# A second norm whose sample columns go through VectorE, a layer set-up that comes earlier, and scalings tied to set steps

## The chip, the cores and the metric

The kernel runs on one core of one Trainium2 chip. The time is that of the device for one execution, in microseconds (us). A core has five engines with instruction streams of their own: TensorE (PE in the profile, with its weight loads shown apart as PEld), VectorE (DVE), ScalarE (ACT), GpSimd (POOL) and SyncE (SP, which here only issues DMAs). Each works through its own stream strictly in order. An instruction that waits for another engine or for a DMA holds up all that stands behind it on its engine.

## The reference

Two layers over 512 prompt tokens and 8 samples of 8 tokens each (64 sample columns), width 1024. Layer 1 is a gated delta rule, layer 2 a differential attention in which keys and values are shared and the samples also read pages of a cache. Around the change this is computed:

```python
def modulate(x, gain, shift, scale):
    return rms_norm(x, gain) * (1 + scale[:, None, :]) + shift[:, None, :]

x = x + gate[:, None, :] * y                     # end of layer 1 (output projection, residual)
h = modulate(x, norm_kv, shift, scale)           # input of k and v
k, v = split(h @ w_kv)
h = modulate(x, norm_b, shift, scale)            # input of q and z
q, z = split(h @ w_in_b)
q = partial_rotary(rms_norm(q), cos, sin)        # the same for k
```

Shift, scale and gate are vectors over the width. The prompt has one set of them, each of the eight samples has its own: so the 512 prompt columns need one scalar per channel, the 64 sample columns a small table of eight per channel.

## The kernel before, in words

Activations lie with channels on the 128 partitions: a tensor such as `x1` is 128 x 8 channel tiles x 576 columns (512 prompt, 64 sample). Every projection is done in two halves of 288 columns; the sample columns are the last 64 of the second half. An operand is split into a high and a low part (`hhi`, `hlo` for activations, `whi`, `wlo` for weights), and three products of the parts are summed (`part`, L238), so one output tile of 128 channels and one half takes 8 x 3 = 24 matmuls. Weights come by SP into `wraw` (L214), ACT rounds them to `whi` (L217), POOL takes the difference `wlo` (L218), about one tile ahead.

The work around the change runs in this order of the program:

1. `out_a` (L1722) finishes the output projection of layer 1, half 0 and then half 1, adds the residual into `x1`, squares it on ACT (L1747), sums the squares on DVE into `rstd` (L1749). `rstd` sits in one of four buffers (`pg`) that later take cache pages.
2. `norm(half)`, inside `out_a`: the sum over partitions on PE (L1731), the reciprocal root by twelve DVE operations (`rsqrt_to`, L181 to L188), and `modulate` (L350), which writes `hhi` and `hlo` for one half. Per channel tile DVE scales (L360), ACT adds the shift and rounds (L362), DVE takes the low part (L363). In the second half each channel tile's 64 sample columns go through three POOL operations (L368 to L370), an ACT copy (L371) and a POOL difference (L372). `norm(0)` runs inside the projection; `norm(1)` is called by `phase_b`.
3. `phase_b` (L2089) starts with the layer's set-up: constants, identity and causal mask in bf16, the lambda of the attention, gains, page table. It has six DMAs on SP and some short DVE, POOL and ACT operations. Then come the cosine and sine tables times the gains (L2156).
4. q projection. Four q tiles (`QH`) get their half 0, with `norm(1)` behind the first; then one block does half 1 of all four, channel tile by channel tile, so 8 x 4 x 3 = 96 matmuls. Four more q tiles follow whole. Every tile is finished by `QKTile.finish`: transposes on PE (L1805, L1807), a copy, squares on ACT (L1810), a sum and a reciprocal root on DVE (L1811 to L172), the rotary part on POOL (L1819 to L1822), transposes back (L1826, L1828), and a last copy to `qT` on ACT and DVE (L1830). Buffers let two finishes run at a time and four tiles wait for theirs.
5. Between the finishes stand three scalings, at places given by `PRE`: `x1` times `rstd` (L2180), the kv input `kT` from it (`scale_shift`, L375, lines L380, L383, L384), and the second use of the q input for z, in place in `x1` (the same lines).
6. `split` (L387) turns `kT` into `hhi` and `hlo` (L393 on ACT, L394 on DVE); then the k tiles, the v tiles and, among them, the samples' pages (`load_page`, L1862, which a POOL copy L1867 and an SP read of its value lead), and the attention.

What sets the order: the first phase's streams are pinned by hand. From `out_a` on a scheduler at compile time orders each engine's stream. It works on simulated time, takes what is ready, and prefers what comes earlier in the program. So a later instruction that is ready stands ahead of an earlier one that isn't, and on the chip that order is fixed. `PRE` therefore gives a place in the program, not a time.

Scratch tiles of 128 x 640 (`scr`) have three buffers in this part.

## Time and profile before

| | |
|---|---|
| time, median of three runs | 1313.99 us (1311.61 to 1315.3) |
| span of the profiled execution | 1313.1 us; it has no other time of its own shown beside the span |
| instructions | 34330 |
| DMA | 240.61 MB, mean 183 GB/s |
| 740 to 760 us (output projection, half 0 and 1) | PE busy 19.11 of 20.00 |
| 800 to 810 us (second norm, second half) | PE busy 6.19 of 10.00, clock 0.56 |
| 840 to 850 us (q tiles) | PE busy 10.00 of 10.00, clock 1.00 |

A row of the timeline gives start and length in us, engine, line, operation, what is written and read with its size, and in brackets how long the engine stood idle before it and who ended that. A matmul's length is that of a pipelined instruction: its successor starts before it ends, so the pace is read from counts over a stretch. In a table of stretches, the columns are the length, then busy time and instruction count of PE, PEld, DVE, ACT and POOL, then the clock granted to PE as a share, the DMA share and GB/s. A row of waits gives the total, the number of times and the longest.

### The profile page before, as it was taken

The numbers are of one execution on the slowest core, as the hardware profiler recorded it, in microseconds if no ns is written. First come the engines' busy times: TensorE is split into PE (matmuls) and PEld (weight loads), VectorE is DVE, ScalarE is ACT, GpSimd is POOL, SyncE is SP. The second block draws the span as 40 slices with busy tenths as digits, with TensorE's granted clock in tenths as the row PEclk, the third lists the DMA queues.
The fourth block names the chain that finished last, engine by engine and source line by source line (L and its number), as shares of the span: only waits on it lengthen the run. The fifth ranks groups of instructions, "written<-read, shape, count | busy, mean of one in ns | idle before, by whom it ended". The sixth has DMA issues, their size and how long they took to land.

```text
span 1313.1 us, 34330 instructions
## 1 busy us (share of the span) xinstructions
PE 1245.7 (95%) x13227; PEld 1083.6 (83%) x13227; DVE 807.7 (62%) x2263; ACT 715.5 (54%) x1981; POOL 444.0 (34%) x811
## 2 busy tenths in 40 slices
...
GB/s 360 133 197 174 157 204 158 195 156 166 200 156 180 153 212 153 189 205 191 226 189 133 163 172 56 81 65 163 297 212 276 213 257 258 284 218 192 93 130 112
DMA packets 86646, 240.61 MB, mean 183 GB/s; under 512 B 14339, under 2 KB 26499, under 8 KB 86483
## 3 DMA queue, kind: packets, MB, share of 16 engines
...
HBM read 212.55 MB, written 25.84 MB: 182 GB/s over the span
## 4 chain that ended last, share of the span: by engine, by line
PE 79%; DVE 6%; DMA 6%; POOL 3%; issue 3%; ACT 2%; SPq 1%; POOLq 0%; DVEq 0%; ACTq 0%
PE pp L437 27%; PE pp L241 14%; PE pa L437 6%; PE pc L437 6%; PE ps L437 2%; PE po L1940 2%; PE pt L437 2%; PE pS L1897 2%; DMA pg<-cv 2%; PE pt L443 2%; PE sc L241 2%; PE pv L2060 1%; DMA pg<-ck 1%; PE sc L2020 1%; DMA araw<-ada 1%
## 5 line engine op out<-in xcount | busy, mean ns | idle before, releaser
L241 PE MATMUL pp<-hhi,whi 128*128 128x288 f32 x640 | 195.0, 308 | 18.8 <-ACT hhi L371 11.9
L241 PE MATMUL pp<-hlo,whi 128*128 128x288 f32 x640 | 193.5, 303 | 2.7 <-DVE hlo L1681 1.9
L241 PE MATMUL pp<-hhi,wlo 128*128 128x288 f32 x640 | 191.7, 301 | 0.2 <-POOL wlo L218 0.2
L437 PE MATMUL pp<-hlo,whi 128*128 128x288 f32 x576 | 166.2, 310 | 0.1
L218 POOL TENSOR_TENSOR wlo<-wraw,whi 128x1024 fp32r<-128x1024 f32 x50 | 120.8, 2419 | 133.3 <-ACT whi L217 115.9
L437 PE MATMUL pp<-hhi,whi 128*128 128x288 f32 x576 | 156.9, 294 | 0.0
L241 PEld LDWEIGHTS pp<-hhi,whi 128*128 128x128 f32 x640 | 121.0, 190 | 27.1 <-ACT hhi L371 12.6
L241 PEld LDWEIGHTS pp<-hlo,whi 128*128 128x128 f32 x640 | 121.7, 190 | 8.1 <-DVE hlo L1681 2.4
L437 PE MATMUL pp<-hhi,wraw 128*128 128x288 f32 x576 | 124.2, 300 | 0.0
L241 PEld LDWEIGHTS pp<-hhi,wlo 128*128 128x128 f32 x640 | 121.7, 190 | 2.3 <-issue 1.7
L437 PEld LDWEIGHTS pp<-hlo,whi 128*128 128x128 f32 x576 | 108.6, 189 | 6.2 <-issue 3.4
L437 PEld LDWEIGHTS pp<-hhi,whi 128*128 128x128 f32 x576 | 108.4, 188 | 0.4
L437 PEld LDWEIGHTS pp<-hhi,wraw 128*128 128x128 f32 x576 | 93.3, 188 | 5.3 <-issue 4.9
L437 PE MATMUL pp<-hhi,wlo 128*128 128x288 f32 x576 | 96.8, 302 | 0.0
L217 ACT CAST whi<-wraw 128x1024 fp32r<-128x1024 f32 x50 | 52.4, 1048 | 77.6 <-PE pp L241 54.4
L970 DVE SCALAR_TENSOR_TENSOR y<-u,vec,y 128x600 f32<-128x600 f32 x96 | 84.9, 884 | 11.4 <-ACT y L967 9.9
L437 PE MATMUL pp<-hlo,wraw 128*128 128x288 f32 x288 | 83.1, 312 | 0.1
L437 PEld LDWEIGHTS pp<-hhi,wlo 128*128 128x128 f32 x576 | 81.2, 188 | 2.1 <-issue 1.2
L790 POOL DMA_DIRECT2D wlo<-wall x37 | 32.9, 889 | 124.2 <-ACT wlo L785 94.3
L2040 DVE TENSOR_REDUCE mx<-sc 128x1 f32<-128x128 f32 (+3 forms) x64 | 31.4, 491 | 60.2 <-PE sc L2022 60.1
L1867 POOL COPY pg<-ptt 1x1 int32<-1x1 int32 x128 | 29.2, 236 | 107.8 <-PE po L1940 46.1
L437 PEld LDWEIGHTS pp<-hlo,wraw 128*128 128x128 f32 x288 | 54.1, 188 | 2.4 <-issue 0.7
...
## 6 DMA issues: line engine op xcount, KB each, us to landing
...
```

The source lines that it names most:

```text
L217: nc.scalar.copy(out=hi[:], in_=raw[:])
L218: nc.gpsimd.tensor_sub(out=lo[:], in0=raw[:], in1=hi[:].bitcast(F32))
L241: K.mm(out=ps[:, :HT], lhsT=w[a][:, k, :], rhs=h[b][:, k, half * HT:half * HT + HT], start=(k == 0 and a + b == 0), stop=(k == 7 and a == 1))
L437: return self.K.nc.tensor.matmul(**kw)
L443: return self.K.nc.tensor.transpose(**kw)
L790: K.nc.gpsimd.dma_start(out=lo[:], in_=src, accum_op=ALU.add)
L970: nc.vector.scalar_tensor_tensor(out=y[:, :YW], in0=u[:, j:j + YW], scalar=cw[j], in1=y[:, :YW], op0=ALU.mult, op1=ALU.add)
L1867: nc.gpsimd.tensor_copy(out=e, in_=P.ptt[0:1, i:i + 1])
L1897: nc.tensor.matmul(out=S[32 * j:32 * j + 32, 128 * pg:128 * pg + 128], lhsT=qs[:, h, :], rhs=kp[:, h, :], start=(hh == 0), stop=(hh == 1), ...
L1940: nc.tensor.matmul(out=po[32 * j:32 * j + 8, hf, :], lhsT=pTs[:, pg, 8 * h:8 * h + 8], rhs=vp[:, h, :], start=False, stop=(pg == NPG - 1 a ...
L2020: nc.tensor.matmul(out=ps[:, :w], lhsT=q[r, m, :], rhs=self.kl[r, 0:w], start=False, stop=False, tile_position=(64 * m, 0))
L2040: nc.vector.tensor_reduce(out=mx[:, m:m + 1], in_=pss[m][:, :w], axis=AX.X, op=ALU.max, negate=True)
```

## The change

Four things are edited.

The second half of the second norm is written by `modulate_rows`. All 8 channel tiles' sample columns together (128 x 512) go through three DVE operations and one ACT copy ahead of the prompt columns, and through a fourth DVE operation behind the first prompt tile. `norm(0)` uses the same function without the sample part. `norm` now returns its last DVE instruction.

The set-up of layer 2 is a function of its own, `setup_b`, called before `out_a`. Two bf16 copies and the memset of `zb` in it are on POOL now, the copies having been on DVE. The cosine and sine tables stay, but are made after `norm(1)`.

Two blocks stand in `tc.issue_after(instruction)`: every instruction traced in the block on that instruction's engine is placed behind it in the stream; no wait is added, and other engines aren't held. The tables go behind the last DVE instruction of `norm(1)`. The three scalings go behind the last DVE instruction (L1830) of the finish of q tile 1, 3 and 6; `PRE` was (1, 5, 6).

`scale_shift` does the sample columns of all channel tiles in two POOL operations in place of sixteen.

```diff
--- before.py
+++ after.py
@@ -372,6 +372,36 @@
                 nc.gpsimd.tensor_sub(out=lo[:, k, SEQ:], in0=tn, in1=hi[:, k, SEQ:].bitcast(F32))
 
 
+def per_sample(t, s):
+
+    return t[:, s, 1:9].unsqueeze(3).to_broadcast([128, 8, NB, DS])
+
+
+def modulate_rows(K, x, rstd, g1, shift_kt, hi, lo, half):
+
+    nc = K.nc
+    n = SEQ - HT if half else HT
+    sl = slice(half * HT, half * HT + n)
+    if half:
+        t = scr(K, 8 * NS).rearrange("p (k n) -> p k n", n=NS)
+        t4 = t.rearrange("p k (b e) -> p k b e", e=DS)
+        nc.vector.tensor_mul(out=t, in0=x[:, :, SEQ:], in1=rstd[:, SEQ:].unsqueeze(1).to_broadcast([128, 8, NS]))
+        nc.vector.tensor_mul(out=t4, in0=t4, in1=per_sample(g1, slice(0, 8)))
+        nc.vector.tensor_add(out=t4, in0=t4, in1=per_sample(K.mod, slice(shift_kt, shift_kt + 8)))
+        nc.scalar.copy(out=hi[:, :, SEQ:], in_=t)
+    for k in range(8):
+        t1 = scr(K, HT)
+        sh = K.mod[:, shift_kt + k, :]
+        nc.vector.scalar_tensor_tensor(out=t1[:, :n], in0=x[:, k, sl], scalar=g1[:, k, 0:1], in1=rstd[:, sl],
+                                       op0=ALU.mult, op1=ALU.mult)
+        nc.scalar.activation(out=hi[:, k, sl], in_=t1[:, :n], func=AF.Identity, bias=sh[:, 0:1])
+        if half and k == 0:
+            nc.vector.tensor_sub(out=lo[:, :, SEQ:], in0=t, in1=hi[:, :, SEQ:].bitcast(F32))
+        last = nc.vector.scalar_tensor_tensor(out=lo[:, k, sl], in0=t1[:, :n], scalar=sh[:, 0:1],
+                                              in1=hi[:, k, sl].bitcast(F32), op0=ALU.add, op1=ALU.subtract)
+    return last
+
+
 def scale_shift(K, xr, g1, shift_kt, out):
 
     nc = K.nc
@@ -379,9 +409,9 @@
         sh = K.mod[:, shift_kt + k, :]
         nc.vector.tensor_scalar(out=out[:, k, 0:SEQ], in0=xr[:, k, 0:SEQ], scalar1=g1[:, k, 0:1], scalar2=sh[:, 0:1],
                                 op0=ALU.mult, op1=ALU.add)
-        xs, os = (a[:, k, SEQ:].rearrange("p (b e) -> p b e", e=DS) for a in (xr, out))
-        nc.gpsimd.tensor_mul(out=os, in0=xs, in1=g1[:, k, 1:9].unsqueeze(2).to_broadcast([128, NB, DS]))
-        nc.gpsimd.tensor_add(out=os, in0=os, in1=sh[:, 1:9].unsqueeze(2).to_broadcast([128, NB, DS]))
+    xs, os = (a[:, :, SEQ:].rearrange("p k (b e) -> p k b e", e=DS) for a in (xr, out))
+    nc.gpsimd.tensor_mul(out=os, in0=xs, in1=per_sample(g1, slice(0, 8)))
+    nc.gpsimd.tensor_add(out=os, in0=os, in1=per_sample(K.mod, slice(shift_kt, shift_kt + 8)))
 
 
 def split(K, t, hi, lo):
@@ -755,7 +785,7 @@
 NV = 0
 WARM = 6
 XW = 2
-PRE = (1, 5, 6)
+PRE = (1, 3, 6)
 SAT = (1, 3, 6)
 FILL = ('vvuv|', 'vvuuu|', 'vuuv|uuuuv', 'huu|', 'zz|u', 'uu|uuzuuu', '|uuuu', 'Zuuuu|zuu', '|uuzZzffff')
 LAST = 'ffffs'
@@ -1730,7 +1760,7 @@
         r = rstd[:, half * HT:half * HT + HT]
         nc.tensor.matmul(out=ps[:, :HT], lhsT=K.ones, rhs=r, start=True, stop=True)
         rsqrt_to(K, r, ps[:, :HT], 1.0 / D, EPS)
-        modulate(K, x1, rstd, K.g1["g1b"], 40, K.hhi, K.hlo, halves=(half,))
+        return modulate_rows(K, x1, rstd, K.g1["g1b"], 40, K.hhi, K.hlo, half)
 
     gain1(K, "norm_b", 48, "g1b")
     with ExitStack() as octx:
@@ -1813,7 +1843,7 @@
         r = rsqrt(K, P.tk, ss[:], 10, tag="rq")
         nc.vector.tensor_mul(out=t[:], in0=t[:], in1=r[:].unsqueeze(2).to_broadcast([128, 10, 64]))
 
-        cos, sin = self.tabs
+        cos, sin = self.tabs[self.out is P.kT]
         rc = P.tk.tile([128, 10, 16], F32, name="rc")
         rsn = P.tk.tile([128, 10, 16], F32, name="rsn")
         nc.gpsimd.tensor_mul(out=rc[:], in0=t[:, :, 0:16], in1=cos)
@@ -1827,15 +1857,15 @@
         pb2 = K.pb.tile([128, 512], F32, name="pb")
         nc.tensor.transpose(out=pb2[:, 0:64], in_=tv[0:64, 4, :], identity=K.ident[0:64, 0:64])
         nc.scalar.activation(out=self.out[:, self.h, :SEQ], in_=pb[:], func=AF.Copy, scale=self.gain)
-        nc.vector.tensor_scalar(out=self.out[:, self.h, SEQ:], in0=pb2[:, 0:64], scalar1=self.gain, scalar2=None,
-                                op0=ALU.mult)
+        return nc.vector.tensor_scalar(out=self.out[:, self.h, SEQ:], in0=pb2[:, 0:64], scalar1=self.gain, scalar2=None,
+                                       op0=ALU.mult).ins
 
 
 def qk_tile(*a):
     t = QKTile(*a)
     t.half(0)
     t.half(1)
-    t.finish()
+    return t.finish()
 
 
 def v_tile(K, P, h):
@@ -2086,43 +2116,34 @@
 LAM_INIT = 0.8 - 0.6 * math.exp(-0.3)
 
 
-def phase_b(K, ctx, x1, rstd, norm_rest):
-    nc = K.nc
-    tc = K.tc
+def setup_b(K, ctx):
+
+    nc = K.nc
     P = Ctx()
-
-    def pool(name, bufs):
-        return ctx.enter_context(tc.tile_pool(name=name, bufs=bufs))
-
-    one = pool("b1", 1)
-    P.pg = K.pg
-    P.ss = pool("bss", 2)
+    one = ctx.enter_context(K.tc.tile_pool(name="b0", bufs=1))
     c = load_con(K, one, K.con_in, "amask", "plain")
     K.comb = c("comb")
     K.m01 = c("m01")
     K.amask = c("amask")
-    K.identb = one.tile([128, 128], BF16, name="identb")[:]
-    nc.vector.tensor_copy(out=K.identb, in_=K.ident)
-    K.cmaskb = one.tile([128, 128], BF16, name="cmaskb")[:]
     cm = scr(K, 128)
     nc.sync.dma_start(out=cm, in_=K.con_in[:, CON["cmask"][0]:CON["cmask"][1]])
-    nc.vector.tensor_copy(out=K.cmaskb, in_=cm)
+    lp = scr(K, 256).rearrange("p (a d) -> p a d", d=64)
+    nc.sync.dma_start(out=lp, in_=K.lp_in.to_broadcast([128, 4, 64]))
+    gc = P.gc = one.tile([128, 2], F32, name="gc")
+    nc.sync.dma_start(out=gc[:], in_=K.gc_in)
+    gr = P.gr = one.tile([128, 2, 16], F32, name="gr")
+    nc.sync.dma_start(out=gr[:], in_=K.gr_in.to_broadcast([128, 2, 16]))
+    P.ptt = one.tile([1, 64], I32, name="ptt")
+    nc.sync.dma_start(out=P.ptt[:], in_=K.pt_in)
+    K.identb = one.tile([128, 128], BF16, name="identb")[:]
+    nc.gpsimd.tensor_copy(out=K.identb, in_=K.ident)
+    K.cmaskb = one.tile([128, 128], BF16, name="cmaskb")[:]
+    nc.gpsimd.tensor_copy(out=K.cmaskb, in_=cm)
+    P.zb = one.tile([128, 128], BF16, name="zb")
+    nc.gpsimd.memset(P.zb[:], 0.0)
     K.sg2 = one.tile([128, 1], F32, name="sg2")
     nc.vector.tensor_scalar(out=K.sg2[:], in0=K.vec[:, VEC["sg"][0]:VEC["sg"][1]], scalar1=0.5 * (1.0 - LAM_INIT),
                             scalar2=None, op0=ALU.mult)
-    P.kT = one.tile([128, 8, NT], F32, name="kT")
-    P.qT = one.tile([128, 8, NT], F32, name="qT")
-    P.qs = [one.tile([128, 8, 32], F32, name=f"qs{i}") for i in range(AHEAD + 1)]
-    P.zb = one.tile([128, 128], BF16, name="zb")
-    for t in P.qs + [P.zb]:
-        nc.gpsimd.memset(t[:], 0.0)
-    P.vn = [one.tile([128, 4, 128], F32, name=f"vn{h}") for h in range(NV)]
-    P.oT = P.qT[:, :, SEQ:].rearrange("p h (b t) -> p h b t", t=8)
-    P.ptt = one.tile([1, 64], I32, name="ptt")
-    nc.sync.dma_start(out=P.ptt[:], in_=K.pt_in)
-
-    lp = scr(K, 256).rearrange("p (a d) -> p a d", d=64)
-    nc.sync.dma_start(out=lp, in_=K.lp_in.to_broadcast([128, 4, 64]))
     l2 = one.tile([128, 4], F32, name="l2")
     nc.vector.tensor_mul(out=lp[:, 0:4:2, :], in0=lp[:, 0:4:2, :], in1=lp[:, 1:4:2, :])
     nc.vector.tensor_reduce(out=l2[:, 0:2], in_=lp[:, 0:4:2, :], axis=AX.X, op=ALU.add)
@@ -2133,37 +2154,53 @@
     P.sgn = one.tile([128, 1], F32, name="sgn")
     nc.vector.scalar_tensor_tensor(out=P.sgn[:], in0=K.m01[:, 1:2], scalar=P.nlam[:, 0:1], in1=K.m01[:, 0:1],
                                    op0=ALU.mult, op1=ALU.add)
-
-    gc = one.tile([128, 2], F32, name="gc")
-    nc.sync.dma_start(out=gc[:], in_=K.gc_in)
-    gr = one.tile([128, 2, 16], F32, name="gr")
-    nc.sync.dma_start(out=gr[:], in_=K.gr_in.to_broadcast([128, 2, 16]))
     for g in (gc[:, 1:2], gr[:, 1, :]):
         nc.vector.tensor_scalar(out=g, in0=g, scalar1=0.125, scalar2=None, op0=ALU.mult)
     nc.vector.scalar_tensor_tensor(out=gc[:], in0=gc[:], scalar=c("plain")[:, 0:1],
                                    in1=c("plain")[:, 1:2].to_broadcast([128, 2]), op0=ALU.mult, op1=ALU.add)
+    return P
+
+
+def phase_b(K, P, ctx, x1, rstd, norm_rest):
+    nc = K.nc
+    tc = K.tc
+
+    def pool(name, bufs):
+        return ctx.enter_context(tc.tile_pool(name=name, bufs=bufs))
+
+    one = pool("b1", 1)
+    P.pg = K.pg
+    P.ss = pool("bss", 2)
+    gc, gr = P.gc, P.gr
+    P.kT = one.tile([128, 8, NT], F32, name="kT")
+    P.qT = one.tile([128, 8, NT], F32, name="qT")
+    P.qs = [one.tile([128, 8, 32], F32, name=f"qs{i}") for i in range(AHEAD + 1)]
+    for t in P.qs:
+        nc.gpsimd.memset(t[:], 0.0)
+    P.vn = [one.tile([128, 4, 128], F32, name=f"vn{h}") for h in range(NV)]
+    P.oT = P.qT[:, :, SEQ:].rearrange("p h (b t) -> p h b t", t=8)
     P.sp = pool("bsp", 1)
     tctx = ExitStack()
     P.tk = tctx.enter_context(tc.tile_pool(name="btk", bufs=2))
     P.ch = tctx.enter_context(tc.tile_pool(name="bch", bufs=QH))
     rot = load_con(K, P.tk, K.con_in, "cos", "sin", 1)
-    tabs = []
-    for i in (1, 0):
-        tab = []
-        for n in ("cos", "sin"):
-            src = rot(n).rearrange("p (c d) -> p c d", d=16)
-            dst = P.tk.tile([128, 10, 16], F32, name=n + "q", bufs=1)[:] if i else src
-            nc.vector.tensor_mul(out=dst, in0=src, in1=gr[:, i, :].unsqueeze(1).to_broadcast([128, 10, 16]))
-            tab.append(dst)
-        tabs.append(tab)
     qctx = ExitStack()
     extra_w(K, qctx, "qx", [("b", h * 128) for h in range(2, QH)])
-    tiles = []
+    tiles, tabs = [], []
     for h in range(QH):
-        tiles.append(QKTile(K, P, ("b", h * 128), h, gc[:, 1:2], tabs[0], P.qT))
+        tiles.append(QKTile(K, P, ("b", h * 128), h, gc[:, 1:2], tabs, P.qT))
         tiles[h].half(0)
         if h == 0:
-            norm_rest()
+            normed = norm_rest().ins
+    with tc.issue_after(normed):
+        for i in (1, 0):
+            tab = []
+            for n in ("cos", "sin"):
+                src = rot(n).rearrange("p (c d) -> p c d", d=16)
+                dst = P.tk.tile([128, 10, 16], F32, name=n + "q", bufs=1)[:] if i else src
+                nc.vector.tensor_mul(out=dst, in0=src, in1=gr[:, i, :].unsqueeze(1).to_broadcast([128, 10, 16]))
+                tab.append(dst)
+            tabs.append(tab)
     pss = [p.tile([128, 512], F32, name=n) for p, n in ((K.pp, "pp"), (K.pp, "pp"), (K.pt, "pt"), (K.pt, "pt"))]
     for k in range(8):
         for t, ps in zip(tiles, pss):
@@ -2172,22 +2209,23 @@
         t.evac(1, ps)
     for h in range(8):
         if h < QH:
-            tiles[h].finish()
+            done = tiles[h].finish()
         else:
-            qk_tile(K, P, ("b", h * 128), h, gc[:, 1:2], tabs[0], P.qT)
-        if h == PRE[0]:
-            for k in range(8):
-                nc.vector.tensor_mul(out=x1[:, k, :], in0=x1[:, k, :], in1=rstd[:])
-        if h == PRE[1]:
-            scale_shift(K, x1, gain1(K, "norm_kv", 32, "g1kv"), 24, P.kT)
-        if h == PRE[2]:
-            scale_shift(K, x1, K.g1["g1b"], 40, x1)
+            done = qk_tile(K, P, ("b", h * 128), h, gc[:, 1:2], tabs, P.qT)
+        with tc.issue_after(done):
+            if h == PRE[0]:
+                for k in range(8):
+                    nc.vector.tensor_mul(out=x1[:, k, :], in0=x1[:, k, :], in1=rstd[:])
+            if h == PRE[1]:
+                scale_shift(K, x1, gain1(K, "norm_kv", 32, "g1kv"), 24, P.kT)
+            if h == PRE[2]:
+                scale_shift(K, x1, K.g1["g1b"], 40, x1)
     samples = [Sample(K, P, b) for b in range(NB)]
     ahead = iter(samples)
     qctx.close()
     split(K, P.kT, K.hhi, K.hlo)
     for h in range(8):
-        qk_tile(K, P, ("kv", h * 128), h, gc[:, 0:1], tabs[1], P.kT)
+        qk_tile(K, P, ("kv", h * 128), h, gc[:, 0:1], tabs, P.kT)
         nc.sync.dma_start(out=K.k_out[h], in_=P.kT[:, h, :])
         if h in SAT:
             next(ahead).pages()
@@ -2396,7 +2434,8 @@
             K.x1p = bctx.enter_context(tc.tile_pool(name="x1p", bufs=1))
             x1 = K.x1p.tile([128, 8, NT], F32, name="x1")
             rstd = K.pg.tile([128, 8, 128], F32, name="pg")[:].rearrange("p a b -> p (a b)")[:, 0:NT]
-            phase_b(K, bctx, x1, rstd, out_a(K, x1, rstd))
+            P = setup_b(K, bctx)
+            phase_b(K, P, bctx, x1, rstd, out_a(K, x1, rstd))
 
 
 def arrays_of(i):
```

## The prediction

> **What bounds the kernel now.** I read the page first: busy time, then the chain that ended last. They say that TensorE (PE) sets the end, so what the change can win is time in which PE stands still or runs at a lowered clock.
>
> ```profile
> PE 1245.7 (95%) x13227; PEld 1083.6 (83%) x13227; DVE 807.7 (62%) x2263; ACT 715.5 (54%) x1981; POOL 444.0 (34%) x811
> PE 79%; DVE 6%; DMA 6%; POOL 3%; issue 3%; ACT 2%; SPq 1%; POOLq 0%; DVEq 0%; ACTq 0%
> ```
>
> So I followed that chain in order of time to where it leaves PE. Between 796 and 826 us it runs through VectorE (DVE) and GpSimd (POOL). The busy time by stage shows the hole and what follows it (columns: length, then busy time of PE, of its weight loads, DVE, ACT and POOL with instruction counts, then clock, DMA share, GB/s):
>
> ```profile
> 796.00:804.00 8.00, 0.47 (x3) 0.33 (x2) 7.79 (x18) 2.20 (x6) 4.75 (x9) 0.67 0.08 33
> 800.00:810.00 10.00, 6.19 (x28) 5.84 (x29) 9.57 (x20) 3.15 (x9) 10.00 (x22) 0.56 0.00 0
> 804.00:827.00 23.00, 17.84 (x97) 16.35 (x97) 15.75 (x31) 5.46 (x16) 22.36 (x58) 0.82 0.00 1
> 827.00:859.00 32.00, 31.17 (x235) 30.35 (x236) 23.27 (x66) 19.10 (x46) 17.23 (x17) 1.00 0.32 99
> ```
>
> The fourth row gives PE's undisturbed pace: 31.17/235 = 0.133 us a matmul. From 796 to 827 PE does 100 matmuls, 13.3 us of work, in 31 us: some 18 us are lost there and only 0.8 in the next 32. Who it waits for, between 788 and 827 and then up to 880 (columns: total, times, longest):
>
> ```profile
> PE pp L241 <- ACT hhi L371: 11.9, 3, 7.5
> PE pt L1807 <- DVE qkt L1808: 1.9, 2, 1.6
> ```
>
> L371 is the copy of the sample columns in the second norm, one per channel tile, behind three POOL operations each. The timelines of the three engines show why it is late:
>
> ```profile
> 789.96 0.45 DVE L181 TENSOR_SCALAR pg<-px 128x288 f32<-128x288 f32 x1
> 791.90 0.29 DVE L2127 TENSOR_TENSOR scr<-scr 128x128 f32<-128x128 f32 x1 [1.50 <-DMA scr<-lp]
> 793.33 0.17 DVE L2142 TENSOR_SCALAR gr<-gr 128x16 f32<-128x16 f32 x1 [0.92 <-DMA gr<-gr]
> 798.16 0.46 DVE L187 TENSOR_TENSOR scr<-scr 128x288 f32<-128x288 f32 x1
> 798.65 0.46 DVE L188 SCALAR_TENSOR_TENSOR pg<-scr,pg 128x288 f32<-128x288 f32 x1
> 804.11 0.50 POOL L383 TENSOR_TENSOR kT<-x,g1kv 128x64 f32<-128x64 f32 x1
> 825.78 0.29 POOL L384 TENSOR_TENSOR x<-x,mod 128x64 f32<-128x64 f32 x1
> 803.67 0.85 PE L241 MATMUL pp<-hhi,whi 128*128 128x288 f32 x2 [7.53 <-ACT hhi L371]
> 826.30 0.29 PE L241 MATMUL pt<-hhi,wlo 128*128 128x288 f32 x1
> ```
>
> Two faults stand in them. The layer's set-up waits for its DMAs in the middle of the reciprocal root (L181 to L188). And from 804 the later scalings (L383, L384 and on DVE L2180, L380) stand between the norm's own steps, since nothing holds them back. After the 7.53 us pause the granted clock is down as well (0.56 in the second row of stages).
>
> **The change part by part.** *Set-up out of the root.* L181 starts at 789.96 and takes a step of 0.37 to its successor; L182 and L183 take 0.3 each, the nine dependent steps 0.49 each (798.16 to 798.65): 5.4 us, so the root is ready at 795.4 and not at 799.1. Gain 3.7 us. If another instruction still slips in, this is 2 us; it can't be below nothing, since the same instructions remain.
>
> *Sample columns in four DVE operations.* Three of 128x512 before the first tile, one after it. The nearest row is 128x640 in 0.82 us (below), so 0.75 each: 2.25 us, then a first scaling, ACT's copy and bias, 0.8 us: PE starts at 798.4. Then DVE needs 2 x 0.43 us a channel tile (the pitch of L360 and L363 there), PE four output tiles x 3 x 0.133 = 1.6 us, so PE sets the pace: 96 x 0.133 = 12.8 us, with 0.8 us for the first low part (among it the fourth operation) ends at 812.0 in place of 826.4. **-14.4 us** for both parts; bounds -16.5 (low parts never late) and -12 (the three operations at a lowered PE clock, 2.4 us).
>
> ```profile
> 805.12 0.49 DVE L360 SCALAR_TENSOR_TENSOR scr<-x,g1b,pg 128x224 f32<-128x224 f32 x1 [0.21 <-POOL hlo L372]
> 851.76 0.82 DVE L1814 TENSOR_TENSOR qkt<-qkt,rqy 128x640 f32<-128x640 f32 x1
> 844.57 0.28 DVE L1830 TENSOR_SCALAR qT<-pb,gc 128x64 f32<-128x64 f32 x1 [1.13 <-PE pb L1828]
> 848.34 0.28 DVE L1830 TENSOR_SCALAR qT<-pb,gc 128x64 f32<-128x64 f32 x1 [0.25 <-PE pb L1828]
> 872.73 0.28 DVE L1830 TENSOR_SCALAR qT<-pb,gc 128x64 f32<-128x64 f32 x1
> 834.65 0.17 DVE L170 TENSOR_TENSOR rqt<-rqy 128x10 f32<-128x10 f32 x1
> 852.50 2.37 DVE L170 TENSOR_TENSOR rqt<-rqy 128x10 f32<-128x10 f32 x1
> 852.26 2.58 POOL L218 TENSOR_TENSOR wlo<-wraw,whi 128x1024 fp32r<-128x1024 f32 x1 [4.61 <-ACT whi L217]
> L2180 DVE TENSOR_TENSOR x<-x,pg 128x576 f32<-128x576 f32 x8 | 6.7, 853 | 0.5 <-POOL scr L368 0.5
> L380 DVE TENSOR_SCALAR kT<-x,g1kv,mod 128x512 f32<-128x512 f32 x8 | 4.1, 537 | 0.0
> 809.66 1.65 DVE L2180 TENSOR_TENSOR x<-x,pg 128x576 f32<-128x576 f32 x2
> 822.75 0.99 DVE L380 TENSOR_SCALAR x<-x,g1b,mod 128x512 f32<-128x512 f32 x2
> DVE qss L1811 <- ACT scr L1810: 5.5, 6, 2.9
> L394 DVE TENSOR_TENSOR hlo<-kT,hhi x16: 445/446/675, 855.3 to 865.8; 128x288 fp32r<-128x288 f32 x16
> 859.08 0.39 ACT L1793 COPY ch<-pp 128x288 f32<-128x288 f32 x1
> ```
>
> *The scalings behind set steps: the cover that goes.* In the hole the scalings (6.7 + 4.1 us on DVE here, 4.1 more for x) cost PE nothing beyond the hole. They now start behind the last DVE instruction of a finish (L1830): x1 times the root behind q tile 1, kT behind tile 3. The kv projection needs kT, and nothing else is left for PE once the eight q tiles are multiplied. That happens at the block's end + 31.5 us (826.4 to 858, when the last q tile's copy at 859.08 is less than a us away and eight kv matmuls are already in): 843.5. When is kT there?
> - Finish of tiles 0 and 1: last L1830 at 848.34, 21.9 after the block; the same chain after the new block: 834.
> - x1 times the root, behind it: 8 steps, 6.4 us at their pitch of 0.80 (two in 1.65), plus one weight split on POOL (L218) beside it. L170 shows what that does: 2.37 us for an operation that takes 0.17 otherwise, as POOL's split runs. 834 + 6.4 + 2.2 = 842.6.
> - Finishes of tiles 2 and 3: in the trace from 848.34 to 872.73, but with 16 splits of kT (L394) and three POOL splits in between. Counting only their own dependent steps (a copy, a square, a reduction, nine root steps of 0.2, a product, 1.9 on POOL, a transpose) it is 9.7 us: 852.3. One more weight split and POOL's merged scalings beside it: 2 to 5 us. I take 855; bounds 845 (finishes at DVE's pace, no collision) and 861 (every collision in full).
> - PE's start of kv: eight scalings of 0.46 (two in 0.99) stand ahead of the first low part, and finishes of tiles 4 and 5 take about half of DVE: I take 4.5 us for what PE can't fill, with a lowered clock in it: PE is as if it began kv at 859.5. Three transposes of finishes (1.8 us) are then done in the pause, and the pauses of 1.9 us behind L1808 and the like need not come again, since the finishes are two tiles ahead: 855.8, against 858 in the trace. So of 14.4 us **+11.7 us** come back.
>
> On this point a rule of the Trainium skill bears ("SBUF — State Buffer", "Who interferes with whom"): a DVE instruction with two SBUF inputs and a GpSimd instruction that reads SBUF exclude each other for a whole instruction. The L170 row agrees (2.37 against 0.17 us). By it the merged scalings on POOL (some 1.2 us each, half of L218's 2.4) hold the root steps up as long as they last; were POOL and DVE to share instead, kT would come some 2 us sooner and the forecast would be 1309.8.
>
> *Merged POOL scalings.* 32 operations of 0.3 to 0.5 us become four of about 1.2 (a 128x1024 split takes 2.4): POOL gains 8 us where it isn't the bound. Nothing on the path, but for the collisions counted above. Scaling x behind q tile 6 costs DVE 4.1 us in a stretch where tiles of 6.4 us PE work need some 5 of DVE: nothing, if the finishes have caught up; 2 if not.
>
> *Set-up ahead of the output projection.* Six DMA issues on SP (0.33 to 0.43 us, 2.2 in all), three POOL operations and some ten short DVE ones go to about 722 us.
>
> ```profile
> 723.01 0.32 SPq L1713 DMA_DIRECT2D x1d<-y  x1
> 725.23 1.27 SPq L1757 DMA_DIRECT2D xin<-x1d  x3
> 726.60 0.37 SPq L214 DMA_DIRECT2D wraw<-wall  x1
> 786.50 0.42 SPq L2291 DMA_DIRECT2D con_amask<-con  x1
> 788.85 0.43 SPq L2140 DMA_DIRECT2D gr<-gr  x1
> PE pb L241 <- ACT whi L217: 1.7, 1, 1.7
> 728.88 1.05 ACT L217 CAST whi<-wraw 128x1024 fp32r<-128x1024 f32 x1 [1.28 <-DVE hlo L1368]
> 730.01 4.77 POOL L218 TENSOR_TENSOR wlo<-wraw,whi 128x1024 fp32r<-128x1024 f32 x2 [4.11 <-DMA wraw<-wall]
> ```
>
> SP stands idle from 723.3 to 725.2, until x1d has landed: there the issues cost nothing. Behind it stands wraw, and at the end of that chain PE waits 1.7 us for whi: what comes between delays PE, up to 2.2 us. DVE queued behind a late DMA could delay the last low parts of the projection's input by as much. I take +0.5; below nothing isn't possible, as nothing there is removed.
>
> The fourth page load needs the root's buffer, now free at 842.6 and not at 820; weights queued behind it on SP and POOL are those of kv tiles 1 and 2, needed after 860: nothing, 2 us if the order puts tile 0's there.
>
> **Sum.** 0.5 - 14.4 + 11.7 = -2.2 us against the profiled span of 1313.1, which lies 0.9 under the median of the runs, 1313.99. Forecast **1311.8 us**. From 0.3%, 3.9 us, a measurement can tell this kernel from no change.
>
> **Rivals.**
> 1. *The cover holds* (faster): the finishes of tiles 0 to 3 are not held up, kT is there at 845, PE goes on with 1 to 2 us of pause. For it: DVE idles 5.5 us waiting for ACT in 829 to 880, which another order could use, and the minimum of the steps is far less than 21.9 us. Against: those 21.9 us are a measured chain that shifts as a whole. Then 10 us of the 11.7 don't come back: about 1303.
> 2. *kT later still* (slower): the second pair of finishes is caught by POOL's merged scalings and two weight splits, kT at 860, PE pauses 16 us in place of 11 at a lowered clock, and the set-up costs its 2.2 us. -2.2 + 5 + 1.7 + 1 = +5.5: 1319.5. It turns slower than before from kT at 857.5 on. The lowered clock is seen after 7.53 us of pause; the Trainium skill ("TensorE: Matmul & The Clock Gate", "What's actually happening") says that an idle window of about 3.4 us suffices, and the trace agrees for the long pause. By that the first pause of 2.3 us costs nothing and the second one does.
> 3. *The change doesn't do what it says*: the root or its first products are still interrupted, by other ready work or by the three operations' own wait, and half of the 14.4 goes without a return: 1313 to 1320.
>
> **How the numbers follow.** My own case 0.44 (1308.5 to 1318), rival 1 0.26, rival 2 0.22, rival 3 0.08. My case lies within 0.3% for 0.30, faster for 0.12, slower for 0.02; rival 3 is split in two. Faster 0.38, same 0.34, slower 0.28. The range takes in the kT bounds: 1302 to 1320.
>
> **What would show it.** The last matmul of the four-tile block lies near 812 and no L383 or L380 before it; a new PE wait of 8 to 14 us for ACT's split of kT (L393) or DVE's (L394) stands between 843 and 860; the scaling of x1 starts near 834. If that wait is under 3 us, rival 1 holds; if it is over 15, rival 2. A first xin load after 727 shows the set-up's price. I would be wrong if the finishes run in another order than they do now, since the planner places them anew.

## The result, and the profile after

The changed kernel took 1327.9 us in the median of 4 runs (1324.8 to 1329.8) against 1314.6 before (1311.6 to 1315.5): a ratio of 1.010, with a 95% interval of 1.007 to 1.013. It is slower by some 13 us; the forecast was 1311.8. Its profiled execution had a span of 1325.7 us, 12.6 above the 1313.1 before, so that this pair of traces shows nearly the whole difference.

To see where the 12.6 us come from, I cut both spans at the same five events: the first step of the root of the last head group of the layer before, the last store of x1d, the first step of the second norm's second root, the end of the first and the end of the fifth finish of a q tile. These are the rows, first of the kernel before (the three others stand in the prediction: 723.01, 789.96 and 844.57), then of the changed one. Columns: start, length, engine, line.

```profile
705.40 0.17 DVE L1319 SCALAR_TENSOR_TENSOR ox<-oms,ssq 128x8 f32<-128x8 f32 x1 [0.56 <-ACT pc L1269]
...
878.32 0.28 DVE L1830 TENSOR_SCALAR qT<-pb,gc 128x64 f32<-128x64 f32 x1
```

```profile
708.03 0.17 DVE L1349 SCALAR_TENSOR_TENSOR ox<-oms,ssq 128x8 f32<-128x8 f32 x1 [0.56 <-ACT pc L1299]
731.50 0.32 SPq L1743 DMA_DIRECT2D x1d<-y  x1
804.05 0.46 DVE L181 TENSOR_SCALAR pg<-px 128x288 f32<-128x288 f32 x1 [0.84 <-PE px L1761]
846.47 0.28 DVE L1860 TENSOR_SCALAR qT<-pb,gc 128x64 f32<-128x64 f32 x1 [1.22 <-PE pb L1858]
891.85 0.28 DVE L1860 TENSOR_SCALAR qT<-pb,gc 128x64 f32<-128x64 f32 x1 [2.97 <-PE pb L1858]
```

The differences of neighbouring rows give six stages. The table holds them for every kernel that was run, in us; "ahead" is the first event's time less 705.4, and all columns add up with 705.4 to the span. "Pit" is the hole of the prediction, from the root's first step over the block of four q tiles to the first finish. How each kernel is made follows below; in the experiments each ratio is to 22 to 31 runs of the kernel before on the same chip. Each profile is of one execution: those of e6, e7, e8 and f2 were the fastest of their kernels' runs, 6 to 9 us under the median, and that of f4 the slowest, 4.8 us above, so that "ahead", "rest" and the span hold for that execution and the ratios for the kernel.

| kernel | ahead | tail | projection | pit | kv | rest | span |
|---|---|---|---|---|---|---|---|
| before | 0 | 17.6 | 67.0 | 54.6 | 33.8 | 434.8 | 1313.1 |
| changed | 2.6 | 23.5 | 72.5 | 42.4 | 45.4 | 433.9 | 1325.7 |
| changed, again (g1) | 2.7 | 23.3 | 70.5 | 42.2 | 44.8 | 436.7 | 1325.6 |
| set-up ahead alone (e2) | 2.0 | 23.1 | 72.4 | 52.0 | 33.7 | 429.5 | 1318.0 |
| the same, light (e8) | 0.4 | 19.3 | 70.8 | 50.4 | 33.8 | 429.3 | 1309.3 |
| changed, set-up back (e1) | 5.4 | 20.5 | 68.6 | 43.8 | 48.8 | 440.0 | 1332.5 |
| changed, lambda back (e4) | 2.7 | 19.3 | 73.7 | 42.4 | 45.0 | 434.8 | 1323.3 |
| changed, page table back (e3) | 2.3 | 23.1 | 68.5 | 42.4 | 49.2 | 440.8 | 1331.7 |
| changed, both back (g2) | 3.0 | 17.6 | 68.0 | 43.1 | 49.0 | 438.4 | 1324.6 |
| rows alone (e7) | -0.1 | 17.6 | 66.8 | 50.1 | 33.8 | 428.7 | 1302.3 |
| ties alone (f2) | -1.4 | 17.6 | 66.2 | 45.1 | 48.2 | 428.4 | 1309.5 |
| changed, kT behind the norm (e5) | 6.0 | 23.3 | 72.4 | 46.4 | 35.6 | 430.8 | 1319.8 |
| changed, columns on DVE (f4) | 5.9 | 23.5 | 72.5 | 42.4 | 42.4 | 434.7 | 1326.8 |
| all behind the norm (e6) | 0.7 | 19.3 | 67.5 | 46.9 | 33.7 | 430.6 | 1304.1 |
| the same, columns on DVE (f1) | 0.5 | 20.5 | 67.3 | 43.6 | 33.8 | 431.4 | 1302.4 |
| the same, set-up free (f3) | 5.0 | 17.6 | 69.2 | 43.9 | 33.8 | 434.2 | 1309.1 |

The second line against the first: +2.6 ahead of the change, +5.9 in the tail, +5.5 in the projection, -12.2 in the pit, +11.6 up to kv, -0.9 in the rest. Tail and projection are where the set-up costs.

**Tail.** In the changed kernel's timeline the product of the lambda parameters (L2148), an instruction of the set-up, stands on VectorE between two steps of the last group's root. It waits 3.08 us for its DMA (SyncE's row); the root's next step stands behind it, then the residual y, and TensorE waits for y.

```profile
707.40 0.73 SPq L2131 DMA_DIRECT2D scr<-lp  x1
...
709.91 0.17 DVE L170 TENSOR_TENSOR rot<-roy 128x10 f32<-128x10 f32 x1
713.16 0.29 DVE L2148 TENSOR_TENSOR scr<-scr 128x128 f32<-128x128 f32 x1 [3.08 <-DMA scr<-lp]
713.37 0.16 DVE L171 TENSOR_TENSOR rot<-rot,roh 128x10 f32<-128x10 f32 x1
```

TensorE's row behind that wait, of before and then of the changed kernel, each with the same 58 matmuls, and the changed kernel's longest waits of TensorE from 690 to 880 (total, times, longest):

```profile
708.35 5.72 PE L450 MATMUL pp<-cT,con_ident 128*128 128x224 bf16 x58 [2.91 <-DVE y L1656]
```

```profile
714.23 8.32 PE L480 MATMUL pp<-cT,con_ident 128*128 128x224 bf16 x58 [6.16 <-DVE y L1686]
```

```profile
PE pp L480 <- DVE y L1686: 6.2, 1, 6.2
PE pb L1856 <- DVE rqt L170: 5.9, 1, 5.9
PE pp L241 <- ACT hhi L391: 3.4, 1, 3.4
PE pp L241 <- ACT hhi L423: 2.8, 2, 2.2
PE pp L241 <- DVE hlo L424: 2.8, 1, 2.8
```

The wait for y grew from 2.91 to 6.16 us, and the 58 matmuls behind it took 8.32 us in place of 5.72, at a granted clock of 0.50 in the first 4 us where it had been 1.00: together the 5.9 us of the tail. Of these the 3.2 us of waiting are the load's; a lowered clock at this place comes without the wait too, as the last section shows. The prediction had looked for the set-up's price behind the last store of x1d (723.01 us before, 731.50 now); the planner put this load at 707.40, ahead of that store by 24 us, and its product with it.

**Projection.** The page table now arrives early, and so the three page loads that wait for it slip in ahead of a weight load (SyncE's timeline):

```profile
745.81 2.75 SPq L1899 DMA_DIRECT2D pg<-ck  x3
748.67 0.37 SPq L214 DMA_DIRECT2D wraw<-wall  x1
```

```profile
740.89 0.40 PE L241 MATMUL pb<-hhi,whi 128*128 128x288 f32 x1 [1.73 <-ACT whi L217]
```

```profile
756.37 0.40 PE L241 MATMUL pb<-hhi,whi 128*128 128x288 f32 x1 [1.81 <-ACT whi L217]
```

The second and third fence have the first matmul of the projection's sixth output tile, of before and of the changed kernel: 15.5 us later, of which 8.5 were there when x1d was stored. Of the 7.0 between, 5.5 are left when the root starts.

The table's cut at the root's first step also counts what VectorE waits for just ahead of it. The projection's own end is TensorE's sum over the partitions, again before and changed:

```profile
789.07 0.75 PE L1731 MATMUL px<-pg,ones 128*128 128x288 f32 x2 [0.69 <-DVE pg L1749]
```

```profile
803.26 0.75 PE L1761 MATMUL px<-pg,ones 128*128 128x288 f32 x2 [0.69 <-DVE pg L1779]
```

From the last store of x1d to there it is 66.1 us before and 71.8 in the changed kernel. Over all sixteen profiles the page table's place parts them: 69.7 to 71.8 in the six that load it ahead (changed, g1, e2, e4, e5, f4), 65.4 to 68.4 in the ten others.

**Pit.** The wait for ACT's sample columns is 3.4 us in place of 11.9 (third of the waits above, against the row in the prediction). First and last matmul of the four-tile block:

```profile
813.72 0.54 PE L241 MATMUL pp<-hhi,whi 128*128 128x288 f32 x2 [3.39 <-ACT hhi L391]
...
828.12 0.29 PE L241 MATMUL pt<-hhi,wlo 128*128 128x288 f32 x1
```

The last one starts 24.1 us behind the root's first step (804.05), in place of 36.3 (826.30 less 789.96). The root itself takes 5.6 us, from 804.05 to the first operation on the sample columns, where it took 9.2 (789.96 to 799.15): 3.6 us won, for the 3.7 of the prediction. But the three operations on the sample columns don't run ahead of the prompt columns, as the program has them: the planner put four operations of the prompt columns between them, which take 1.4 us (VectorE's timeline).

```profile
809.67 0.69 DVE L388 TENSOR_TENSOR scr<-x,pg 128x512 f32<-128x512 f32 x1
810.28 0.81 DVE L395 SCALAR_TENSOR_TENSOR scr<-x,g1b,pg 128x224 f32<-128x224 f32 x2
...
811.61 0.81 DVE L400 SCALAR_TENSOR_TENSOR hlo<-scr,mod,hhi 128x224 fp32r<-128x224 f32 x2
812.33 0.68 DVE L390 TENSOR_TENSOR scr<-scr,mod 128x512 f32<-128x512 f32 x1
```

**kv.** TensorE's busy time by stage shows the pause that was forecast, at a clock of 0.65 and 0.50, and VectorE with nothing to do 40 us earlier:

```profile
810.00:820.00 10.00, 6.61 (x37) 6.22 (x36) 9.05 (x24) 4.33 (x10) 0.00 (x0) 0.83 0.00 0
820.00:830.00 10.00, 8.95 (x66) 8.48 (x64) 0.00 (x0) 2.82 (x7) 1.70 (x1) 1.00 0.01 2
...
860.00:870.00 10.00, 3.53 (x15) 2.54 (x15) 8.62 (x22) 2.83 (x6) 5.57 (x9) 0.65 0.39 139
870.00:880.00 10.00, 3.73 (x12) 2.50 (x12) 9.96 (x22) 7.20 (x19) 4.78 (x4) 0.50 0.00 0
```

The scalings stand where the ties put them (VectorE's timeline): x1 times the root behind the finish of tile 1, kT behind that of tile 3.

```profile
831.15 0.69 DVE L1838 COPY qkt<-pt 128x512 f32<-128x512 f32 x1 [11.91 <-PE pt L1835]
...
850.15 0.28 DVE L1860 TENSOR_SCALAR qT<-pb,gc 128x64 f32<-128x64 f32 x1 [0.27 <-PE pb L1858]
850.35 5.43 DVE L2218 TENSOR_TENSOR x<-x,pg 128x576 f32<-128x576 f32 x8
855.70 2.38 DVE L171 TENSOR_TENSOR rqt<-rqt,rqh 128x10 f32<-128x10 f32 x1
871.93 6.01 DVE L410 TENSOR_SCALAR kT<-x,g1kv,mod 128x512 f32<-128x512 f32 x8
```

The first row shows VectorE empty for 11.91 us right behind the norm; the finish of tile 1 ends at 850.15, 22.0 us behind the block. The row at 855.70 is a root step of 0.17 us that POOL's weight split holds up, as in the prediction's row at 852.50.

The pause has two parts. TensorE runs out of q tiles at 859.95, 31.5 us behind the block, as forecast. Its longest wait, 5.9 us, is then for the finish of tile 2 (L1856 in the list above), whose root steps the scaling of x1 and two weight splits have held up; only behind it come 5.6 us for the split of kT (L423 and L424).

How far the stage's length is the loss is seen from the matmuls in it (the table of stretches, from the first to the fifth finish, before and changed):

```profile
844.57:878.32 33.75, 31.88 (x236) 30.46 (x237) 30.24 (x80) 19.48 (x46) 16.46 (x18) 1.00 0.20 63
```

```profile
846.47:891.85 45.38, 32.37 (x200) 29.24 (x201) 39.34 (x98) 17.86 (x42) 22.46 (x24) 0.77 0.15 47
```

The changed kernel does 36 matmuls fewer there, 4.8 us at the pace of 0.133. At equal work the loss is therefore 16.4 us and not 11.6, and counted in the same way it is 16.4 at the last store of k too. The rest then has those 36 more and is still 0.9 shorter, so 5.7 us come back behind the k tiles, at a granted clock of 0.99 where it was 0.98. Whether that is the change or the single execution isn't settled.

### The profile page after: what moved, and what is told of

It is laid out like the page before. It is cut to its first block, busy times and chain, and to the rows that moved or that the text cites. A ratio compares the mean times of both kernels' runs of the same rounds, so it can differ in the third digit from the quotient of the medians.

```text
span 1325.7 us, 34258 instructions
## 1 busy us (share of the span) xinstructions
PE 1248.2 (94%) x13227; PEld 1086.5 (82%) x13227; DVE 803.7 (61%) x2265; ACT 713.7 (54%) x1974; POOL 420.2 (32%) x753
## 4 chain that ended last, share of the span: by engine, by line
PE 82%; DVE 8%; DMA 5%; ACT 3%; issue 2%; SPq 1%; POOL 0%; POOLq 0%; DVEq 0%; ACTq 0%
PE pp L467 27%; PE pp L241 16%; PE pa L467 6%; PE pc L467 6%; PE po L1970 2%; PE pS L1927 2%; PE ps L467 2%; PE pt L467 2%; PE sc L241 2%; PE pt L473 2%; PE sc L2050 2%; PE pv L2090 2%; PE pp L480 1%; PE pt L241 1%; DMA araw<-ada 1%
## 5 line engine op out<-in xcount | busy, mean ns | idle before, releaser
L1000 DVE SCALAR_TENSOR_TENSOR y<-u,vec,y 128x600 f32<-128x600 f32 x96 | 84.9, 884 | 11.1 <-ACT y L997 9.6
```

The lines of the kernel that those rows point to most:

```text
L1000: nc.vector.scalar_tensor_tensor(out=y[:, :YW], in0=u[:, j:j + YW], scalar=cw[j], in1=y[:, :YW], op0=ALU.mult, op1=ALU.add)
```

## The experiments

Theories at the start: **late kT** (the ties make kT late, +12) and **early set-up** (the set-up's loads ahead of the projection cost the larger part); later, that the sample columns or the ties win the pit.

### Is it the set-up?

Three kernels take it apart: the change without the set-up's move (e1), the move alone (e2), and the move alone without the lambda parameters and the page table (e8).

```diff
# e1, on the changed kernel
-            P = setup_b(K, bctx)
-            phase_b(K, P, bctx, x1, rstd, out_a(K, x1, rstd))
+            norm_rest = out_a(K, x1, rstd)
+            P = setup_b(K, bctx)
+            phase_b(K, P, bctx, x1, rstd, norm_rest)
# e2, on the changed kernel: norm, scalings and their order as before, set-up ahead
-        return modulate_rows(K, x1, rstd, K.g1["g1b"], 40, K.hhi, K.hlo, half)
+        modulate(K, x1, rstd, K.g1["g1b"], 40, K.hhi, K.hlo, halves=(half,))
-        with tc.issue_after(done):
-PRE = (1, 3, 6)
+PRE = (1, 5, 6)
# e8, on e2, in setup_b
-    lp = scr(K, 256).rearrange("p (a d) -> p a d", d=64)
-    nc.sync.dma_start(out=lp, in_=K.lp_in.to_broadcast([128, 4, 64]))
...
-    P.ptt = one.tile([1, 64], I32, name="ptt")
-    nc.sync.dma_start(out=P.ptt[:], in_=K.pt_in)
# and in phase_b
     gc, gr = P.gc, P.gr
+    P.ptt = one.tile([1, 64], I32, name="ptt")
+    nc.sync.dma_start(out=P.ptt[:], in_=K.pt_in)
+    lp = scr(K, 256).rearrange("p (a d) -> p a d", d=64)
+    nc.sync.dma_start(out=lp, in_=K.lp_in.to_broadcast([128, 4, 64]))
...
```

In e2 the scalings and the tables are also free of their ties again, and POOL scales the sample columns channel by channel; in e8 the six operations on lp (L2148 to L2155) move with it.

Expected of e1:

> Two theories. 'Early set-up': what costs the time is the set-up's new place, some 14 us up to the start of the second norm (a VectorE wait for the lambda parameters inside the last step of layer 1, six issues on SP, and page loads ahead of weights), while the norm and the scalings behind set steps about cancel (-13.5 and +12). 'Late kT': the scalings behind the finishes cost more than the norm gains, whatever the set-up does. Here the set-up is called behind the output projection again and all else is as in the changed kernel. Early set-up expects 1328 - 14 + 1 to 4 us, since the set-up's waits stand in the norm's root again: 1315 to 1318. Late kT expects 1325 to 1328.

Expected of e2:

> The kernel before with one part of the change, the set-up ahead of the output projection; norm, scalings and their order as before. Early set-up expects +14 us up to the second norm and -3.7 us from a root without the set-up's waits in it: 1314.6 + 10 = 1325 (1322 to 1329). Late kT expects no loss, rather a small gain from the root: 1311 to 1315.

Expected of e8:

> The run with the set-up ahead alone (1321), less the lambda parameters and the page table, which go back behind the output projection. If these two are the set-up's price (a VectorE wait for the parameters between two root steps of the last group, three page loads ahead of a weight load): 1314-1316. If it is the rest (issues ahead of the first input of the projection, an order of matmuls planned anew): 1319-1322.

Measured: e2 1321.3 us, ratio 1.0059 (1.0027 to 1.0091); e8 1316.8, ratio 1.0012 (0.9981 to 1.0042); e1 1334.5, ratio 1.0156 (1.0119 to 1.0194), in 4 runs.

e2 and e8 lie just outside the ranges that they come nearest to (1322 to 1329 and 1314 to 1316). So the move alone costs some 7 us, and without the two loads nothing that can be told from noise; the two intervals overlap a little, and it is the stages that part the kernels. In the table e2 has the changed kernel's tail and projection within 0.4 us (23.1 and 72.4); e8 has 19.3 and 70.8. Of e8's 70.8, 1.5 us are a new wait: its lambda parameters are late again, and VectorE waits for them just ahead of the root's first step. Up to TensorE's sum it takes 68.4, so that 2.4 us above the kernel before remain without either load. All six profiles with the lambda parameters ahead have a tail of 23.1 to 23.5, all ten others one of 17.6 to 20.5. In return both kernels win 2.6 to 4.2 us in the pit, since the root takes 5.6 us in both in place of 9.2, without a wait inside it.

e1 fell against both theories: with the set-up back it should have been faster than the changed kernel, or as fast, and was slower. The two loads, one at a time and together in the changed kernel, were to say why.

The edits are those lines of e8's diff, on the changed kernel: e4 moves lp with its operations, e3 moves ptt, g2 both.

Expected of e4:

> The changed kernel, with only the lambda parameters' DMA and the operations on them behind the output projection. If their wait on VectorE costs 3.3 us and the lowered TensorE clock behind it 2.6 us, less up to 3.7 us as they stand in the norm's root again: 1322 to 1326. If the loss is elsewhere, 1327 to 1332.

Expected of e3:

> The changed kernel, with only the page table's buffer and DMA behind the output projection again, so that no page can be loaded there. If three early page loads ahead of a weight load cost 5.6 us, 1328 - 5.6 = 1322 (1320 to 1324). If the pages are not the cause, 1326 to 1329.

Expected of g2:

> The changed kernel, less the lambda parameters and the page table, which go back behind the output projection; the scalings stay tied behind the q tiles. Terms add up: the projection's +5.5 falls to 2 to 4, the tail's +2.6 to 0 to 2, the block stays at -12, kT is late by 11.6 to 15 us: 1316-1321. If the set-up's issues and its matmul order are the price, whatever is loaded: 1325-1329.

Measured: e4 1322.7, ratio 1.0078 (1.0046 to 1.0110); e3 1329.2, ratio 1.0100 (1.0072 to 1.0129); g2 1329.3, ratio 1.0088 (1.0056 to 1.0121).

In the trace the lambda parameters behave as said: the tail is 19.3, 4.2 us less, of which 1.2 come back as a wait ahead of the root. e4's median is in the range expected for that, 5 us under 1327.9, but its interval overlaps that of the changed kernel (1.0073 to 1.0129), so that the gain in time is likely and not shown. The page table behaves so only up to the root: e3 saves 4.0 us in the projection, where 5.6 were expected, and then has 3.8 more in kv and 6.9 more in the rest. The same is seen in g2 (projection -4.5, kv +3.6, rest +4.5) and in e1 (-3.9, +3.4, +6.1). The longer kv is no loss: between the two finishes TensorE does 231 or 232 matmuls in e1, e3 and g2, and 200 in the changed kernel, g1 and e4. The 31 more are 4.1 us of work, which the planner put ahead of the fifth finish, and at the last store of k these kernels lie within 1 us of the changed one at equal work. What e3 saved is lost behind the k tiles. There the granted clock is 0.97 or 0.98 in e1, e3 and g2 and 0.99 in the changed kernel and g1, and in e3 TensorE waits 4.8 us for pages of the keys (pg<-ck) in place of 1.6. Why is open; f2, which also has both the ties and a late page table, has 0.99 there and a rest of 428.4. So e1's 1334.5 is located but not explained.

To see whether the changed kernel's own numbers hold, it was run once more.

Expected of g1:

> The changed kernel as it is, in more runs and with a second profile. In its first profile the stages that the change touches account for +6.6 us (tail of the layer before +2.6, projection +5.5, block of q tiles -12.2, q tiles to kv +11.6, after that -0.9), and +5.9 was there ahead of them, where the program's order is the same. If that part is a matter of the clock in the single run, the second profile shows the same terms within 1 us and the median lies nearer 1321; if it belongs to this program, the second profile shows it again and the median stays at 1326-1330.

Measured: 1328.4, ratio 1.0086 (1.0054 to 1.0119) in 12 runs, and the same stages within 0.6 us up to kv, but for the projection (70.5 for 72.5); the rest is 2.8 longer. The median stayed high. My text for this run cut one event later: of its +5.9 "ahead", 3.2 are the lambda wait, which also stands ahead of the last but one store of x1d; 2.6 to 2.7 remain, twice the same, at a place where the order of work is that of before. More on them in the last section.

### What wins the pit?

```diff
# e7, on the kernel before
-        modulate(K, x1, rstd, K.g1["g1b"], 40, K.hhi, K.hlo, halves=(half,))
+        modulate_rows(K, x1, rstd, K.g1["g1b"], 40, K.hhi, K.hlo, half)
# f2, on the kernel before
-PRE = (1, 5, 6)
+PRE = (1, 3, 6)
-            tiles[h].finish()
+            done = tiles[h].finish()
+        with tc.issue_after(done):
             if h == PRE[0]:
...
```

Expected of e7:

> The kernel before, with only the sample columns in four VectorE operations: set-up, scalings and their order by readiness stay. If the three POOL operations a channel tile were the pit: the block of four q tiles ends near 815 in place of 826, kT stays in the pit with the other scalings, and the time is 1302-1305. If the scalings that are ready at the same time take the norm's place on VectorE, so that the pit needs the set order: the block ends near 822, 1309-1313. No change or slower: the pit is VectorE's total work, whatever its form.

Expected of f2:

> The kernel before, with only the scalings tied behind the finishes of q tiles 1, 3 and 6. Late kT: the pit loses the scalings (the block of four q tiles ends 4 to 8 us sooner) and kv pays 12: 1319-1323. If kT is late only because the block's end and the finishes come sooner in the changed kernel: 1314-1317.

Measured: e7 1311.8, ratio 0.9976 (0.9942 to 1.0010), so that a gain is likely but not certain; f2 1320.3, ratio 1.0047 (1.0026 to 1.0068).

Four VectorE operations alone take 4.5 us from the pit, the ties alone 9.5, all three parts 12.2. In e7's timeline of VectorE the scalings still stand between the norm's operations:

```profile
804.51 0.88 DVE L395 SCALAR_TENSOR_TENSOR scr<-x,g1b,pg 128x224 f32<-128x224 f32 x2
805.32 0.54 DVE L410 TENSOR_SCALAR x<-x,g1b,mod 128x512 f32<-128x512 f32 x1
805.77 0.68 DVE L399 TENSOR_TENSOR hlo<-scr,hhi 128x512 fp32r<-128x512 f32 x1
806.38 0.54 DVE L410 TENSOR_SCALAR x<-x,g1b,mod 128x512 f32<-128x512 f32 x1
```

So it was the work that was ready at the same time, more than POOL's three operations a channel, that made the pit. f2 shows the price by itself: kv 48.2 in place of 33.8, more than the pit won.

### Is late kT needed?

In e5 the two scalings that kv needs follow the norm's last low part, where VectorE had nothing to do.

```diff
# e5, on the changed kernel
     with tc.issue_after(normed):
         for i in (1, 0):
             ...
+        for k in range(8):
+            nc.vector.tensor_mul(out=x1[:, k, :], in0=x1[:, k, :], in1=rstd[:])
+        scale_shift(K, x1, gain1(K, "norm_kv", 32, "g1kv"), 24, P.kT)
...
-            if h == PRE[0]:
-                for k in range(8):
-                    nc.vector.tensor_mul(out=x1[:, k, :], in0=x1[:, k, :], in1=rstd[:])
-            if h == PRE[1]:
-                scale_shift(K, x1, gain1(K, "norm_kv", 32, "g1kv"), 24, P.kT)
# e6, on e5
-    cm = scr(K, 128)
+    cm = one.tile([128, 128], F32, name="cm")[:]
-    lp = scr(K, 256).rearrange("p (a d) -> p a d", d=64)
+    lp = one.tile([128, 4, 64], F32, name="lp")[:]
...
     with tc.issue_after(normed):
+        setup_rest(K, P)
         for i in (1, 0):
...
-            phase_b(K, P, bctx, x1, rstd, out_a(K, x1, rstd))
+            phase_b(K, P, bctx, x1, rstd, norm_rest)
```

In e6 setup_b stands behind out_a, as in e1, and setup_rest is the part of it from K.sg2 on.

Expected of e5:

> The changed kernel with one difference: x1 times the root and the scaling into kT follow the norm's last low part on VectorE, not the finishes of q tiles 1 and 3. Late kT (the planned place of the scalings makes kT late, and TensorE idles for it): VectorE did nothing from 819 to 831 us in the changed kernel, the 10 us of scalings fit in there, the waits of TensorE at the start of kv (5.9 + 2.8 + 2.8 + 1.3 us) shrink to under 3, and the time falls by 10 to 12 from 1328 to 1316-1318. Rival, VectorE short of time: the scalings push the finishes of the q tiles back by as much as they come sooner, TensorE waits for the finishes in place of kT, 1325 or more.

Expected of e6:

> As the run before, and the set-up's DMAs are issued behind the output projection, where the kernel before has them, while its VectorE operations follow the norm's last low part; the two loaded constants lie in buffers of their own, so that they hold none of the root's. If the three terms add up (set-up ahead costs 7, late kT 12, the sample columns and the undisturbed root win 13): 1300-1304, faster than the kernel before by 10 to 14. If the set-up's place does not matter: 1316, as the run before. If the late page table costs the sample stage as much as the early one cost the projection: 1308-1312.

Measured: e5 1319.7, ratio 1.0026 (0.9994 to 1.0058); e6 1311.9, ratio 0.9960 (0.9934 to 0.9987).

Late kT stands: kv falls from 45.4 to 35.6 and 33.7, and no wait of TensorE between 840 and 905 is over 2 us. But the pit grew by 4 us, to 46.4 and 46.9, so that e5 came out above the 1316 to 1318 expected and e6 above the 1300 to 1304 at which the three terms would have added up. (e6 lies in the range that I had given to a late page table, but its rest of 430.6 is not longer than before.) VectorE's and POOL's timelines of e5 say why:

```profile
827.70 1.45 DVE L410 TENSOR_SCALAR kT<-x,g1kv,mod 128x512 f32<-128x512 f32 x1
827.78 1.08 POOL L413 TENSOR_TENSOR kT<-x,g1kv 128x512 f32<-128x512 f32 x1
831.37 2.46 POOL L218 TENSOR_TENSOR wlo<-wraw,whi 128x1024 fp32r<-128x1024 f32 x1
831.53 2.59 DVE L410 TENSOR_SCALAR kT<-x,g1kv,mod 128x512 f32<-128x512 f32 x1
```

Both of VectorE's scalings shown end 0.29 us behind the POOL operation beside them. All eight, with the merged POOL operations and two weight splits beside them, took 11.1 us, against 4.1 in the kernel before. So in the next pair the merged operations move to VectorE.

```diff
# f1 on e6, f4 on the changed kernel, in scale_shift
-    nc.gpsimd.tensor_mul(out=os, in0=xs, in1=per_sample(g1, slice(0, 8)))
-    nc.gpsimd.tensor_add(out=os, in0=os, in1=per_sample(K.mod, slice(shift_kt, shift_kt + 8)))
+    nc.vector.tensor_mul(out=os, in0=xs, in1=per_sample(g1, slice(0, 8)))
+    nc.vector.tensor_add(out=os, in0=os, in1=per_sample(K.mod, slice(shift_kt, shift_kt + 8)))
```

f3 is f1 with set-up as in e1: behind out_a, lp and cm in scr, and its VectorE operations not tied.

Expected of f1:

> The run with all behind the norm (1311.9), with the sample columns of kT and of x scaled by two VectorE operations each in place of two POOL ones. Exclusion (while POOL's merged operation reads and writes SBUF, VectorE's scalings of kT wait): the eight scalings took 11.1 us in one run and about as long in the other, against 4.1 in the kernel before; with 1.5 us of VectorE operations in POOL's place they take 4.1 + 1.5, the finishes of the first q tiles come 4 to 5 us sooner, and the time is 1306-1308. Rival, plain total of VectorE: the scalings stay at 10 us or the gain there is lost at the next wait: 1311-1313.

Expected of f4:

> The changed kernel, with the sample columns of kT and x on VectorE in place of POOL. Exclusion: the eight scalings of kT take 4 us in place of 6.0, kT is there 0 to 1 us sooner (the two VectorE operations cost 1.5), and the time stays within 2 us of 1328. If POOL's merged operations hold up the finishes too: 1322-1325. Late kT itself predicts that the wait of TensorE for kT stays above 8 us.

Expected of f3:

> As the first run of these four, but the set-up as the kernel before has it: its VectorE operations are free to stand in the norm's root. If the set-up in the root costs what the prediction said (3.7 us of the root): 3 to 4 us above the first run. If the order by readiness finds room for it anyway: within 1 us of the first run.

Measured: f1 1306.8, ratio 0.9943 (0.9923 to 0.9963); f4 1323.9, ratio 1.0055 (1.0039 to 1.0071); f3 1309.8, ratio 0.9958 (0.9940 to 0.9975).

```profile
815.05 0.55 DVE L410 TENSOR_SCALAR kT<-x,g1kv,mod 128x512 f32<-128x512 f32 x1
815.57 3.29 DVE L410 TENSOR_SCALAR kT<-x,g1kv,mod 128x512 f32<-128x512 f32 x7
818.76 0.69 DVE L413 TENSOR_TENSOR kT<-x,g1kv 128x512 f32<-128x512 f32 x1
```

In f1 the eight take 3.8 us, the pit is 43.6 with kT inside it, and the only waits of TensorE between 840 and 905 are the two old ones of the finish:

```profile
PE pt L1837 <- DVE qkt L1838: 1.9, 2, 1.6
```

f1 is faster than both kernels, than the one before by some 7 us (5 to 10 by the interval). e6's interval overlaps f1's, so that it is the pit, 3.3 us shorter, and not the time that shows what the move to VectorE is worth; POOL's two weight splits there now take 6.78 us in place of 5.1 in e6. f4's median is 4 us under the changed kernel's, in the range that I had given to the other case, that the finishes are held up too; but its pit is unchanged at 42.4 and the gain of 3.0 lies in kv, with 199 matmuls for 200, so it is the scalings that came sooner (3.7 us for 6.0). I had also written that TensorE's wait for kT would stay above 8 us; it is 4.0, behind the same 5.9 for the finish. f3 is 3.0 us above f1, but their intervals overlap; its trace has 1.9 us more in the projection, of which 1.2 are the set-up's waits for DMAs just ahead of the root, and 0.3 in the pit. That agrees in size with the 3.7 us that the prediction gave for the root, and does not settle it.

## Why the prediction was wrong

The forecast was a sum of three terms. The mechanism of two held, with one of them mis-sized; the third failed.

- *Pit, -14.4 (bounds -12 to -16.5):* measured -12.2 from the root's first step to the first finish, and -12.3 to the block's end (24.1 us for 36.3). TensorE started 9.7 us behind the root's first step (8.4 forecast) and needed 14.7 for the block (13.6). The late start is the prompt columns' operations between those on the sample columns. The first matmul came after a pause of 3.4 us, and the mean clock from 810 to 820 was 0.83, which the forecast had in its lower bound and not in its value. Within bounds. Its attribution was less good: I wrote of two faults and costed the columns first; e7 and f2 show that the ties do most of it.
- *kT cover, +11.7:* the stage is 11.6 us longer, in the second profile 11.0, but that this meets the forecast is in part luck of the cut: at equal work it is 16.4, of which 5.7 come back later, and kv and rest together have 10.7. The mechanism is right. The chain shifted as a whole, as the row of 21.9 us had it; the scaling into kT began at 871.93, 43.8 us behind the block's last matmul (43). What was too small is the size: from a pause of 16 us (843.5 to 859.5) the prediction took off 3.7 for transposes done in it and for pauses that need not come again, as the finishes would be two tiles ahead. They weren't: the transposes of tile 2 were the first thing that TensorE waited for, and the wait of 8 to 14 us for the split of kT that the prediction named as its sign came as 5.6 behind 5.9. Rival 1, that the cover holds, is refuted: e5 shows that VectorE had the room, but the ties kept it from using it. Rival 2 did not come in its cause, as kT was at its forecast place, though the loss at equal work is nearer to its figure. Of rival 3 a small part came: the root ran undisturbed, but other ready work stood between the three operations (1.4 us). Rival 1's own sum gives 1301.8, 11.8 less 10, where the prediction wrote about 1303.
- *Set-up, +0.5 (bounds 0 to 2.2):* **this is the step that failed.** Measured: +11.4 in the first profile (tail 5.9, projection 5.5), +9.2 in the second, and +7.2 us in the time of e2, which has this part alone and the shorter root with it. Of the 11.4, 3.2 are the wait for the lambda parameters, 2.6 the lowered clock behind it, which can come without it, 4.0 the page table by e3; the 1.5 that remain lie within the bounds. I had counted the issues on SyncE and one late DMA in front of VectorE's low parts. I had not asked what the early data would set free: the lambda product became ready, to the planner, inside the last root of the layer before and waited there for its load; and the page table let three page loads go ahead of a weight load. I followed the moved DMAs past their queue, and not the instructions that wait for them. The bound was built at one place, 723 us, though nothing fixed the place.
- *Sum:* -12.2 + 11.6 + 11.4 = +10.8, with 2.6 ahead of the change and -0.9 behind: 12.5, for 12.6 between the spans. With the measured set-up in place of +0.5 the forecast's own sum would have been -14.4 + 11.7 + 11.4 = +8.7, or 1322.7. Between the forecast's -2.2 and the 12.6 of the spans lie 14.8 us: 10.9 are the set-up, 2.2 the pit and 2.6 what lies ahead of the change, less 1.0 in kv and the rest.
- The rule of the Trainium skill that the prediction weighed ("SBUF — State Buffer", "Who interferes with whom") agrees with the rows, and I used too little of it. The same section of the Trainium skill says that `tensor_scalar` can enter a mode in which it takes the shared ports too; by that the scalings of kT themselves wait for POOL, and e5's rows of 1.45 and 2.59 us, against 0.54 without POOL, agree. The prediction gave them 0.46 each.
